# Other distances between the steps of the attention and mLSTM chains, matrix sums in threes, and another order of the first late sets in a hybrid decoder layer

## The chip, the cores and the metric

The kernel runs on one core of a Trainium2 chip. The metric is the device time of one execution in microseconds (us); the time before is the median of three runs. The trace is one profiled execution of the kernel before. Engines are called by the profile's names: PE multiplies matrices, PEld is its weight load, DVE and ACT do vector and scalar work, POOL a part of the vector work and some transfers, SP issues most transfers.

## What is computed

One decoder layer on 2048 tokens of width 1024, with 16 learned meta tokens in front. One input projection feeds two branches, which are gated, merged and projected:

```python
proj = u @ w_in
(a_q, a_k, a_v, a_z, m_qk, m_v, m_i, m_f, m_o, m_z, g_a, g_m) = split(proj)
att = sliding_window_attention_with_sinks(a_q, a_k, a_v)      # 16 heads, window 128, rope
y_a = (att * silu(a_z)) @ w_attn_out
m_q, m_k = split(silu(causal_conv(m_qk)))
cell = mlstm(m_q, m_k, m_v, m_i, m_f)                         # 4 heads, running state
hm = head_layernorm(sigmoid(m_o) * cell)
y_m = (hm * silu(m_z)) @ w_mlstm_out
out = rmsnorm((sigmoid(g_a) * y_a + sigmoid(g_m) * y_m) @ w_out) + x
```

All of it is float32. The kernel splits an operand into a high and a low part and multiplies three times (high by high, high by low, low by high).

## The kernel before

**Stage 1** goes through the tokens in two halves (c = 0 and 1) of 8 blocks of 128. In each half a plan lists projections: four times an A block (8 projections of q, k and v of a group of heads, `token_proj`, L756), an F block (4 projections for the mLSTM's q and k, `feat_proj`, L768) and an M block (8 projections of v and the output gate of an mLSTM head, L756 again); after the second and the fourth there is a block G of gates. A projection is 24 matmuls, of 512 columns in F and M and of 384 or 392 in A.

Between them stand the steps of **chains**, Python generators that a function `slot()` advances. A slot comes after each 6 projection matmuls: three within a projection, one behind it. What a generator yields is the number of slots until its next step. So the order on PE is written out by hand; the orders on DVE, ACT, POOL and SP come from a scheduler.

An **attention chain** treats a block of tokens and a group of heads. A new one starts every 12 slots at the earliest:

- three transposes of q and k (L440); ACT and DVE split them into `qs` and `ks` (L443 to L449);
- after `ATT_YIELDS[0]` slots the scores of the first two heads (L467, four matmuls into the tile `s`, two banks, one buffer); DVE masks (L469) and takes the row bounds (L473, L474), ACT takes the exponentials (L476) and thereby frees `s`;
- after `ATT_YIELDS[1]` slots the scores of the other two heads into the same buffer, L467 again;
- after `ATT_YIELDS[2]` slots the transposes of P (L492 and, for the meta columns, L493); ACT L496 and DVE L497 split them into `pc`, POOL masks (L501, L504) and spreads the meta part (`pmb`, L510);
- after `ATT_YIELDS[3]` slots P times V (L519, up to five matmuls); the result is stored to `att_d`.

In an M block each of 8 projections starts an **mLSTM chain**: a step T1 (L613 a transpose of k, L614 k times q) with its decay weights `dws` (ACT L627, DVE L628); after `ML_YIELDS[0]` slots the product with the state and the state's update (L587: six matmuls into `acc`, three into `su`, read by DVE L636); after `ML_YIELDS[1]` slots two transposes of the result (L652), which ACT L653 copies out.

L440, L492, T1, `su`, L652 and the meta keys' transposes (L411, L412) share one **PSUM pool of two buffers**, the tiles `tr`: each use waits until the engine that reads the use before the last is done with that buffer.

At the ends of the A blocks with index 1 and 3 the loop calls `slot()` without any matmul between the slots (**bare slots**) until enough chains are done: 57 of 813 slots.

`attn_meta` prepares the meta keys of a group once in each of the four A blocks of the first half: POOL turns them (rope, L281 to L284) and, after a `yield`, PE transposes them (L411, L412). `weight_sums` adds pairs of weight blocks in DRAM for the late stage, by transfers issued on ACT (`cp`) and POOL (`add`, L171), one per slot, with six matrices in all; some steps read what an earlier one has written.

**The late stage** has 12 sets (`SETS`), each with 7 products (`PRODS`) of 48 matmuls of 512 columns (L1144): a seven-product scheme for blocks of 2 by 2. A set's operands come from DRAM and are split by ACT (L965) and DVE (L966) into `st` and `r`; the tiles `r` of the tokens (from `uo_d`) are split in the first set of a half alone. A set's results go through a chain of DVE operations (L1035 to L1044, L1095 to L1100), much shorter for `gm` than for `az` and `mz`.

Of the kernel before, what the change touches and what calls it, by code (L numbers as in the profile page):

```python
# [35 lines left out]
NHALF = NB // HALF_BLOCKS  # L36
SBH = HALF_BLOCKS * 128 // SB
BIG = 1e30
ATT_YIELDS = (5, 5, 8, 9)
ML_YIELDS = (4, 6)  # L40
CHAIN_PHASE = 2
DMA_LEAD = 30
SPLIT_LEAD = 2
# [41 lines left out]
MATS = ("az", "mz", "gm", "att", "hm", "out")  # L85
# [3 lines left out]
def hybrid_layer(ctx: ExitStack, tc: tile.TileContext, x, xT, mx, mxT, gpre, w_all, wq, negs, cw, cb,  # L89
# [5 lines left out]
    def pool(name, bufs=1, space=None, es=ctx):  # L95
        kw = {} if space is None else {"space": space}
        return es.enter_context(tc.tile_pool(name=name, bufs=bufs, **kw))
# [16 lines left out]
    def f(t):  # L114
        return t.bitcast(F32)
# [62 lines left out]
                yield  # L178

    def weight_sums():  # L180
        for a in range(0, len(MATS), 2):
            pair = (a, a + 1)
            for op, i, src in ((cp, 2, (0, 0)), (cp, 0, (1, 1)), (add, 2, (0, 1)), (add, 0, (0, 1)),
                               (cp, 1, 2), (add, 1, (1, 1)), (cp, 3, 1), (add, 3, (1, 0))):
                for m in pair:
                    for j in range(2):
                        cs = slice(j * 2 * SB, (j + 1) * 2 * SB)
                        v = sw_d[m][src] if isinstance(src, int) else wq[m, src[0], src[1]]
                        op(sw_d[m][i][:, cs], v[:, cs])
                        yield  # L190
# [45 lines left out]
    with es1:  # L236
# [3 lines left out]
        def wt(name, shape, dt=F32, bufs=None):  # L240
            kw = {} if bufs is None else {"bufs": bufs}
            return wk.tile(shape, dt, name=name, **kw)
# [20 lines left out]
        def meta_proj(wh, wl, c0, n, dst):  # L263
            ps = ps_a.tile([128, SB], F32, name="acc")
            i = 0
            for k in range(KT):
                for w in (wh[k], wl[k]):
                    T.matmul(ps[0:48, :n], lhsT=um[:, k, :], rhs=w[:, c0:c0 + n],
                             start=(i == 0), stop=(i == 2 * KT - 1))
                    i += 1  # L270
            tmp = stage.tile([128, SB], F32, name="xs")
            S.copy(tmp[:NM, :n], ps[32:32 + NM, :n])
            tt(dst, ps[0:NM, :n], tmp[:NM, :n], ALU.add)

        def apply_rope(view, pos, nh, p):
            c = rope_t[:p, pos:pos + 1, 0:16].broadcast_to([p, nh, 16])
            sn = rope_t[:p, pos:pos + 1, 16:24].broadcast_to([p, nh, 8])
            sp = rope_t[:p, pos:pos + 1, 24:32].broadcast_to([p, nh, 8])
            a = wt("ropa", [128, 6, 16], bufs=1)
            b = wt("ropb", [128, 6, 16], bufs=1)  # L280
            G.tensor_tensor(a[:p, :nh], view[:, :, 0:16], c, ALU.mult)  # L281
            G.tensor_tensor(b[:p, :nh, 0:8], view[:, :, 8:16], sn, ALU.mult)
            G.tensor_tensor(b[:p, :nh, 8:16], view[:, :, 0:8], sp, ALU.mult)
            G.tensor_tensor(view[:, :, 0:16], a[:p, :nh], b[:p, :nh], ALU.add)  # L284
# [116 lines left out]
        def attn_meta(g, wh, wl, gt_raw):  # L401
            n = 136 if g == 0 else 128
            kv = stage.tile([128, SB], F32, name="xs")[:NM, 0:200]
            meta_proj(wh, wl, 256, n, kv[:, 64:64 + n])
            if g == 0:
                V.tensor_copy(gt_raw[0:NM, 0, :], kv[:, 192:200])
            V.tensor_copy(kv[:, 0:64], kv[:, 64:128])
            apply_rope(kv[:, 0:128].rearrange("p (a d) -> p a d", a=2), NB, 2, NM)
            yield 4
            tr = ps_t.tile([128, SB], F32, name="tr")  # L410
            T.transpose(out=tr[:, 0:NM], in_=kv[:, 0:128], identity=ident_t[:NM, :NM])  # L411
            T.matmul(tr[:, 64:128], lhsT=sel_t, rhs=kv[:, 128:192], start=True, stop=True)  # L412
            S.copy(KM[g][:, 0], tr[:, 0:NM])
            tt(KM[g][:, 1], tr[:, 0:NM], f(KM[g])[:, 0], ALU.subtract)
            S.copy(VM[g][:, 0:64], tr[:, 64:128])
            tt(VM[g][:, 64:128], tr[:, 64:128], f(VM[g])[:, 0:64], ALU.subtract)
# [20 lines left out]
        def attn_block(g, b, qkv, vt, vp, last):  # L437
# [18 lines left out]
            kring[0] = ks  # L456
            yield ATT_YIELDS[0]
            P = wt("P", [128, 4, 144], bufs=2)
            mn = wt("mn", [128, 16])
            c0 = 0 if b > 0 else 128  # L460
            for pr in range(2):
                if pr == 1:
                    yield ATT_YIELDS[1]
                sp = ps_s.tile([128, 2, SB], F32, name="s")
# [22 lines left out]
            tt(Pv[:, :, :, NM:], Pv[:, :, :, NM:], rv.broadcast_to([128, 2, 2, 128]), ALU.mult)  # L487
            yield ATT_YIELDS[2]
            tm = ps_a.tile([128, SB], F32, name="acc")
# [13 lines left out]
            for i in range(2):  # L503
# [7 lines left out]
                            bm_t.rearrange("p (s a) -> p s a", a=1).broadcast_to([128, 4, 128]), ALU.mult)  # L511
            yield ATT_YIELDS[3]
            ops = [(VM[g], pmb), (vt.rearrange("p a d -> p (a d)"), pc[:, 0]),
# [90 lines left out]
        def mlstm_chain(h, b, j, v1, tho, qT, kT, GT, mrep):  # L604
# [23 lines left out]
            tt(dws[:, 1], dw, f(dws)[:, 0], ALU.subtract)  # L628
            yield ML_YIELDS[0]
            acc = ps_a.tile([128, SB], F32, name="acc")  # L630
# [17 lines left out]
            S.activation(tho, tho, AF.Identity, bias=sm[:, 13:14], scale=sm[:, 11:12])  # L648
            yield ML_YIELDS[1]
            th = ps_t.tile([128, SB], F32, name="tr")  # L650
# [137 lines left out]
        u = [None, None]  # L788
        late = None
        sums.append(weight_sums())  # L790

        def first_proj(us, wh, wl, w):
# [12 lines left out]
        for c in range(NHALF):  # L805
# [7 lines left out]
            for pi, (kind, arg, cols) in enumerate(PLAN):  # L813
# [24 lines left out]
                if kind == "A":  # L838
                    chains = []
                    for i in range(HALF_BLOCKS):  # L840
# [28 lines left out]
                        if c == 0 and i == 6:  # L869
                            start(attn_meta(arg, wh, wl, gt_raw))  # L870
# [39 lines left out]
                else:  # L910
# [25 lines left out]
                    if un:  # L936
                        u = un
# [11 lines left out]
    NPAIR = SEQ // (2 * SB)  # L949
# [3 lines left out]
    ring = pool("ring", 1)  # L953
    ps_1 = pool("ps_1", 4, PSUM)
    ps_0 = pool("ps_0", 4, PSUM)
    SETS = [(n, c, ("u", c)) for c in range(NPAIR) for n in ("az", "mz", "gm")]
    SETS += [(n, c, ("w", n)) for n in ("att", "hm", "out") for c in range(NPAIR)]
    OPD = {"att": "att", "hm": "hm", "out": "mg"}
    IDX = {"P1": 0, "P2": 1, "P6": 2, "P5": 3, "P7": 4, "P3": 5, "P4": 6}

    def split(pl, nm, src, p, sign=1.0, bufs=None):
        raw = src.pop(0)
        op = pl.tile([128, 2, 2, SB], R, name=nm, **({} if bufs is None else {"bufs": bufs}))
        if sign == 1.0:
            S.copy(op[:, 0], raw)  # L965
            tt(op[:, 1], raw, f(op)[:, 0], ALU.subtract)  # L966
        else:
            S.activation(op[:, 0], raw, AF.Copy, scale=sign)
            stt(op[:, 1], raw, sign, f(op)[:, 0], ALU.mult, ALU.subtract)
        return op  # L970

    def weight_src(n, name):
        m = MATS.index(n)
        v = sw_d[m][int(name[1]) - 1] if name[0] == "s" else wq[m, int(name[1]), int(name[2])]
        return v.rearrange("p (k n) -> p k n", k=4)

    N = len(SETS) * NP
    fetched, ready, resident = {}, {}, {}

    def fetch(n):  # L980
        u, i = divmod(n, NP)
        nm, c, key = SETS[u]
        w_src = weight_src(nm, PRODS[i][2])
        b_src = (uo_d[c] if key[0] == "u" else op_d[OPD[nm], c])[i]
        srcs = [w_src, b_src] if key[0] == "u" else [b_src, w_src]
        if u and SETS[u - 1][2] == key:
            srcs.pop()
# [7 lines left out]
    def prep(n):  # L995
# [3 lines left out]
        if raws:  # L999
            sign = -1.0 if SETS[u][2][0] == "u" and PRODS[i][0] == "P6" else 1.0  # L1000
            resident[i] = [split(res if i else first, f"r{i}{p}", raws, p, sign) for p in range(2)]
# [119 lines left out]
    for n in range(N):  # L1121
        u, i = divmod(n, NP)
        nm, c, key = SETS[u]
        name, bset = PRODS[i][0], (PRODS[i][1] + u) % 2
# [94 lines left out]
```

## Time and profile before

| | us |
|---|---|
| median of three runs | 2472.01 (2469.97 to 2474.32) |
| the profiled execution, own time | 2472.98 |
| its span in the trace | 2469.8 |
| PE busy | 2305.6 (93%) |
| DVE, ACT, POOL busy | 1565.6, 1135.5, 635.0 |

The span is the time from the first to the last instruction that the profile shows; the execution's own time holds 3.2 us more. The granted clock (PEclk) is TensorE's as a share of full speed: 0.50 is 1.2 GHz, 1.00 is 2.4 GHz, and a stretch between them had a part at either. An idle time in square brackets stands before the instruction of its row, with what ended it.

### The profile page before, as it was taken

How to read it: one execution, taken by the hardware profiler on the slowest of the kernel's cores; microseconds unless marked ns; L12 is line 12 of the kernel's file. 1: busy time of each engine (PE TensorE's matmuls, PEld its weight loads, DVE VectorE, ACT ScalarE, POOL GpSimd, SP SyncE). 2: the span in 40 equal slices, each digit the busy share in tenths (PEclk: the TensorE clock that was granted, in tenths of full speed). 3: DMA queues.
4: the chain of work that ended last, by engine and by line, in shares of the span. 5: the costliest groups of instructions: out<-in, count | busy, mean ns of one | idle time of the engine just before them, and what ended most of it. 6: DMA issues, size and time to landing. Idle time of an engine off the chain costs nothing.

```text
span 2469.8 us, 34243 instructions
## 1 busy us (share of the span) xinstructions
PE 2305.6 (93%) x11149; PEld 1942.8 (79%) x11149; DVE 1565.6 (63%) x3371; ACT 1135.5 (46%) x2785; POOL 635.0 (26%) x1347
## 2 busy tenths in 40 slices
PE   7998889898998999999999997999999999989897
PEld 6787779687787878778788885788878888877686
DVE  7866654565766765754767755765587463666675
ACT  6554543454554454543555544444543442333342
POOL 5244344245342436343344430000000000000010
PEclk9999999999999999999999998999999999999999
DMA  7325445634468637445411117866797676889974
GB/s 231 126 63 147 97 94 114 150 90 122 98 152 224 167 91 140 107 94 122 120 46 56 43 48 238 285 228 221 253 296 222 212 258 214 283 272 304 285 264 151
DMA packets 216915, 415.51 MB, mean 168 GB/s; under 512 B 23212, under 2 KB 80896, under 8 KB 216736
## 3 DMA queue, kind: packets, MB, share of 16 engines
q1 hardware_dynamic: 200032, 352.51, 44.0%
q0 software_dynamic: 9792, 35.66, 9.7%
q10 hardware_dynamic: 6912, 25.17, 3.4%
q8 instruction: 87, 1.43, 0.2%
q14 instruction: 92, 0.75, 0.1%
HBM read 302.06 MB, written 172.00 MB: 192 GB/s over the span
## 4 chain that ended last, share of the span: by engine, by line
PE 41%; DVE 10%; DMA 8%; issue 3%; ACT 3%; POOL 2%; SPq 1%; ACTq 0%; DVEq 0%; POOLq 0%
PE x L1144 25%; PE pj L756 7%; PE pj L768 5%; DMA raw<-uo_d 2%; DMA wraw<-in_w_all 2%; PE acc L519 1%; DMA ld<-gm_d 1%; DVE st L966 1%; PE s L467 1%; DVE wlo L213 1%; DVE e L1085 1%; DMA raw<-sw_d 1%; DVE xs L531 1%; DMA hm_d<-tho 1%; ACT P L476 1%
## 5 line engine op out<-in xcount | busy, mean ns | idle before, releaser
L1144 PE MATMUL x<-r,st 128*128 128x512 f32 x2688 | 619.8, 393 | 29.2 <-DMA ld<-att_d 13.1
L756 PE MATMUL pj<-whi,un 128*128 128x512 f32 (+2 forms) x1952 | 636.1, 383 | 0.0
L1144 PEld LDWEIGHTS x<-r,st 128*128 128x128 f32 x2688 | 509.7, 190 | 139.4 <-ACT st L965 13.8
L756 PEld LDWEIGHTS pj<-whi,un 128*128 128x128 f32 x1952 | 375.1, 194 | 41.9 <-issue 2.3
L756 PE MATMUL pj<-wlo,un 128*128 128x512 f32 (+2 forms) x976 | 365.8, 375 | 4.7 <-DVE wlo L213 4.7
L768 PE MATMUL pj<-un,whi 128*128 128x512 f32 x1024 | 328.1, 402 | 1.2 <-ACT xs L542 1.2
L966 DVE TENSOR_TENSOR st<-raw,st 128x1024 fp32r<-128x1024 f32 x168 | 204.4, 1222 | 189.1 <-ACT st L965 182.5
L1144 PE MATMUL x<-st,r 128*128 128x512 f32 x1344 | 308.8, 392 | 9.1 <-DVE st L966 5.3
L965 ACT CAST st<-raw 128x1024 fp32r<-128x1024 f32 x168 | 176.2, 1052 | 290.6 <-PE x L1144 155.3
L1144 PEld LDWEIGHTS x<-st,r 128*128 128x128 f32 x1344 | 253.6, 189 | 64.2 <-DVE st L966 6.0
L1052 POOL TENSOR_TENSOR yss<-yss,mhalf 128x1 f32<-128x1 f32 x16 | 12.6, 795 | 959.1 <-DVE yss L1051 954.3
L768 PEld LDWEIGHTS pj<-un,whi 128*128 128x128 f32 x1024 | 188.6, 192 | 36.8 <-ACT xs L542 1.6
L756 PEld LDWEIGHTS pj<-wlo,un 128*128 128x128 f32 x976 | 190.5, 195 | 24.5 <-DVE wlo L213 7.9
L768 PE MATMUL pj<-un,wlo 128*128 128x512 f32 x512 | 202.8, 396 | 0.0
L476 ACT ACTIVATE P<-s,mn 128x144 f32<-128x144 f32 x256 | 95.2, 378 | 170.6 <-DVE mn L474 161.8
L213 DVE TENSOR_TENSOR wlo<-wraw,whi 128x512 fp32r<-128x512 f32 (+3 forms) x224 | 142.1, 657 | 27.2 <-ACT whi L212 26.2
L966 DVE TENSOR_TENSOR r<-raw,r 128x1024 fp32r<-128x1024 f32 x66 | 80.6, 1223 | 106.6 <-ACT r L965 106.4
L501 POOL TENSOR_SCALAR_AFFINE_SELECT pp<-pc 128x512 fp32r<-128x512 f32 x120 | 77.4, 646 | 247.1 <-ACT pc L496 240.2
L212 ACT CAST whi<-wraw 128x512 fp32r<-128x512 f32 (+3 forms) x224 | 110.8, 529 | 54.0 <-DMA wraw<-in_w_all 43.4
L965 ACT CAST r<-raw 128x1024 fp32r<-128x1024 f32 x66 | 69.4, 1051 | 116.5 <-DMA raw<-uo_d 45.6
L768 PEld LDWEIGHTS pj<-un,wlo 128*128 128x128 f32 x512 | 97.8, 191 | 21.9
L469 DVE COPY_PREDICATED s<-um,s 128x256 f32<-128x256 int32 x120 | 51.0, 425 | 98.2 <-PE s L467 97.8
(365 smaller groups left out, 3609.2 us busy)
## 6 DMA issues: line engine op xcount, KB each, us to landing
raw<-sw_d SPq DMA_DIRECT2D x72, 512.0 KB, 5.8
raw<-in_wq SPq DMA_DIRECT2D x54, 512.0 KB, 4.5
wraw<-in_w_all SPq DMA_DIRECT2D x96, 256.0 KB, 3.9
sw_d<-in_wq POOLq DMA_DIRECT2D x48, 512.0 KB, 7.3
raw<-uo_d SPq DMA_DIRECT2D x28, 512.0 KB, 4.9
raw<-op_att_d SPq DMA_DIRECT2D x28, 512.0 KB, 5.5
raw<-op_hm_d SPq DMA_DIRECT2D x28, 512.0 KB, 6.0
raw<-op_mg_d SPq DMA_DIRECT2D x28, 512.0 KB, 5.3
```

What stands on the lines that cost most here:

```text
L212: S.copy(hi[:, :w], raw[:, :w])
L213: tt(lo[:, :w], raw[:, :w], f(hi)[:, :w], ALU.subtract)
L467: T.matmul(sp[:, pa, c0:272], lhsT=qs[:, pr, pa, :], rhs=ks[:, i, c0:272], start=(i == 0), stop=(i == 1))
L469: V.copy_predicated(sp[:, :, 144:272], um_t.rearrange("p (a t) -> p a t", a=1).broadcast_to([128, 2, 128]), sp[:, :, 0:128] if b > 0 else ...
L476: S.activation(P[:, 2 * pa + pr], sp[:, pa, 128:272], AF.Exp, bias=mn[:, 2 * pr + pa:2 * pr + pa + 1], scale=-1.0, accum_out=mn[:, 4 + 2 * ...
L501: G.affine_select(pp[:, i], f(pc)[:, i], pattern=[[0, 4], [-1, 128]], compare_op=ALU.is_gt, fill=0.0, base=0, channel_multiplier=1)
L519: T.matmul(acc, lhsT=l, rhs=r.rearrange("p s q -> p (s q)"), start=(i == 0), stop=(i == len(ops) - 1))
L756: T.matmul(ps[:, :w], lhsT=us[k][:, a, o:o + 128], rhs=ww[k][:, :w], start=(n == 0), stop=(n == 3 * KT - 1))
L768: T.matmul(ps, lhsT=ww[k][:, 128 * i:128 * i + 128], rhs=us[k][:, a], start=(n == 0), stop=(n == 3 * KT - 1))
L965: S.copy(op[:, 0], raw)
L966: tt(op[:, 1], raw, f(op)[:, 0], ALU.subtract)
L1144: T.matmul(banks[bset][g], lhsT=l, rhs=r, start=(fresh and p == 0 and kk == 0 and m == 0), stop=(p == 1 and kk == 1 and m == 2), skip_grou ...
```

## The change

Six lines change. Of the attention chain's distances the first grows by two slots, the second shrinks by two and the third grows by one; both distances of the mLSTM chain shrink by one. `weight_sums` goes through three matrices at once (the variable is still called `pair`). The meta keys' transposes come 8 slots behind their rope instead of 4. In the first half the late sets run gm, az, mz.

```diff
-ATT_YIELDS = (5, 5, 8, 9)
-ML_YIELDS = (4, 6)
+ATT_YIELDS = (7, 3, 9, 9)
+ML_YIELDS = (3, 5)
...
     def weight_sums():
-        for a in range(0, len(MATS), 2):
-            pair = (a, a + 1)
+        for a in range(0, len(MATS), 3):
+            pair = range(a, a + 3)
...
             apply_rope(kv[:, 0:128].rearrange("p (a d) -> p a d", a=2), NB, 2, NM)
-            yield 4
+            yield 8
...
-    SETS = [(n, c, ("u", c)) for c in range(NPAIR) for n in ("az", "mz", "gm")]
+    SETS = [(n, c, ("u", c)) for c in range(NPAIR) for n in (("az", "mz", "gm") if c else ("gm", "az", "mz"))]
```

The first place is PE in the first M block of the second half, around the q and k transposes (L440) of an attention chain. `su` is written by the L587 that name `tr`, `DVE_49` and `Activation_49` are semaphores of those engines. Before:

```order
L587 MATMUL tr<-v_7605,kw 128x258 [waits PE_49]
L587 MATMUL tr<-v_7605,kw 128x258 x2
L613 MATMUL tr<-ident,kT 128x128
L614 MATMUL tr<-qT,kT 128x128
L756 MATMUL pj<-whi,un 128x512
L756 MATMUL pj<-wlo,un 128x512
L756 MATMUL pj<-whi,un 128x512 x2
L756 MATMUL pj<-wlo,un 128x512
L756 MATMUL pj<-whi,un 128x512
L440 MATMUL tr<-ident,qkv 128x128 [waits DVE_49]
```

The same chains in the changed kernel:

```order
L587 MATMUL tr<-v_7629,kw 128x258 [waits PE_49]
L587 MATMUL tr<-v_7629,kw 128x258 x2
L756 MATMUL pj<-whi,un 128x512
L756 MATMUL pj<-wlo,un 128x512
L756 MATMUL pj<-whi,un 128x512 x2
L756 MATMUL pj<-wlo,un 128x512
L756 MATMUL pj<-whi,un 128x512
L652 MATMUL tr<-ident,tho 128x128 x2
L613 MATMUL tr<-ident,kT 128x128 [waits DVE_49]
L614 MATMUL tr<-qT,kT 128x128
L440 MATMUL tr<-ident,qkv 128x128 [waits Activation_49]
```

T1 has moved from behind `su` to one slot later, into the slot of L652 and L440; L440, which waited for DVE's reading of `su` over 6 projection matmuls, now waits for ACT's copy of the L652 two rows above it. Such a wait of L440 stands in 14 places of the changed kernel.

The second place is PE at the end of the second A block of the second half, where bare slots begin. Before:

```order
L467 MATMUL s<-ks,qs 128x272 [waits DVE_49,PE_49,Activation_49]
L467 MATMUL s<-ks,qs 128x272 x3
L756 MATMUL pj<-whi,un 128x384
L756 MATMUL pj<-wlo,un 128x384
L756 MATMUL pj<-whi,un 128x384 x2
L756 MATMUL pj<-wlo,un 128x384
L756 MATMUL pj<-whi,un 128x384
L440 MATMUL tr<-ident,qkv 128x128 x3
L519 MATMUL acc<-pmb,vm_197 128x512 [waits Pool_49]
```

In the changed kernel:

```order
L492 MATMUL tr<-ident,P 128x128 x4
L493 MATMUL acc<-ident,Pm 64x128 [waits Pool_49]
L467 MATMUL s<-ks,qs 128x272 [waits Activation_49]
L467 MATMUL s<-ks,qs 128x272 [waits DVE_49]
L467 MATMUL s<-ks,qs 128x272 x2
L756 MATMUL pj<-whi,un 128x384
L756 MATMUL pj<-wlo,un 128x384
L756 MATMUL pj<-whi,un 128x384 x2
L756 MATMUL pj<-wlo,un 128x384
L756 MATMUL pj<-whi,un 128x384
L467 MATMUL s<-ks,qs 128x272 [waits DVE_49,PE_49,Activation_49]
L467 MATMUL s<-ks,qs 128x272 x3
```

Between the transposes of P and the P·V behind these rows (L519) stood 30 projection matmuls before, and 6 now; both pairs of scores of the next chain have come in between. The same holds at the end of the fourth A block of that half. In the whole of stage 1, 66 of 822 slots are bare.

The third place is DVE in the late stage at the end of the set `mz` of the first half, where the splits of the next set's operands (L966) follow the last operations on results. Before, with `gm` as the next set:

```order
L1095 SCALAR_TENSOR_TENSOR th<-th,x 128x512
L966 TENSOR_TENSOR st<-raw,st 128x1024
L1100 SCALAR_TENSOR_TENSOR bt<-ld,hn,th 128x512
L966 TENSOR_TENSOR st<-raw,st 128x1024
L1044 SCALAR_TENSOR_TENSOR b_18150<-b_18150,bt 128x512
L966 TENSOR_TENSOR st<-raw,st 128x1024 x3
```

In the changed kernel, with `az` of the second half next:

```order
L1095 SCALAR_TENSOR_TENSOR th<-th,x 128x512 x2
L1100 SCALAR_TENSOR_TENSOR bt<-ld,hn,th 128x512 x2
L1044 SCALAR_TENSOR_TENSOR b_18639<-b_18639,bt 128x512
L1044 SCALAR_TENSOR_TENSOR b_18648<-b_18648,bt 128x512
L966 TENSOR_TENSOR st<-raw,st 128x1024 x2
L966 TENSOR_TENSOR r_18891<-raw,r_18891 128x1024
L966 TENSOR_TENSOR r_18894<-raw,r_18894 128x1024
L966 TENSOR_TENSOR st<-raw,st 128x1024 x2
```

The splits have moved behind the last L1100 and L1044, and two splits of `r` stand among them.

## Rows read from the trace of the kernel before

**Rows 1.** Two stretches: busy per engine (instructions), granted clock, DMA share, GB/s

```profile
0.00:1489.00 1489.00, 1377.35 (x7117) 1179.54 (x7117) 952.19 (x2571) 738.99 (x2241) 622.38 (x1331) 0.96 0.45 115
...
1502.20:2194.00 691.80, 685.51 (x3001) 565.96 (x3002) 422.15 (x521) 297.14 (x386) 0.00 (x0) 0.99 0.75 246
```

**Rows 2.** Waits of PE, 0 to 1490: who for whom, total, times, longest

```profile
PE tr L613 <- DVE pc L497: 14.5, 11, 2.9
PE tr L411 <- POOL xs L284: 14.4, 4, 4.4
PE acc L519 <- POOL pmb L510: 13.8, 5, 4.2
PE tr L613 <- DVE ks L449: 8.8, 4, 3.4
PE s L467 <- ACT ks L448: 7.9, 4, 4.6
...
PE tr L440 <- DVE cst L636: 5.6, 7, 1.8
PE s L467 <- ACT P L476: 4.9, 3, 2.8
...
PE s L467 <- DVE ks L449: 2.3, 4, 1.0
```

**Rows 3.** A stretch of 16 us around a P·V wait, columns as in rows 1

```profile
192.00:208.00 16.00, 12.90 (x68) 12.05 (x67) 8.55 (x23) 5.88 (x25) 5.47 (x12) 0.79 0.35 109
```

**Rows 4.** Two stretches of 16 us around waits of T1 and L467

```profile
484.00:500.00 16.00, 13.25 (x55) 10.36 (x56) 9.74 (x28) 6.82 (x21) 4.93 (x10) 0.79 0.30 62
...
756.00:772.00 16.00, 11.41 (x50) 9.53 (x50) 6.67 (x17) 4.76 (x13) 3.60 (x6) 0.89 1.05 321
```

**Rows 5.** The same columns, 1210 to 1226

```profile
1210.00:1226.00 16.00, 10.67 (x53) 8.07 (x52) 10.79 (x29) 7.46 (x26) 5.65 (x10) 1.00 0.27 80
```

**Rows 6.** Timeline of PE: start, duration, line, operation, count [idle before <- releaser]

```profile
1081.93 0.33 PE L613 MATMUL tr<-ident,kT 128*128 128x128 f32 x1 [1.59 <-DVE pc L497]
...
1083.03 0.62 PE L768 MATMUL pj<-un,whi 128*128 128x512 f32 x2
...
1083.72 0.62 PE L768 MATMUL pj<-un,whi 128*128 128x512 f32 x2
```

**Rows 7.** L652: count, min/median/max ns, first and last start

```profile
L652 PE MATMUL tr<-ident,tho x128: 270/271/473, 119.8 to 1446.8; 128*128 128x128 f32 x128
```

**Rows 8.** L653, the copy behind it, same columns

```profile
L653 ACT COPY tho<-tr x64: 347/372/380, 121.1 to 1447.2; 128x256 f32<-128x256 f32 x64
```

**Rows 9.** L467, the scores

```profile
L467 PE MATMUL s<-ks,qs x512: 228/288/594, 81.6 to 1469.2; 128*128 128x272 f32 x160, 128*128 128x144 f32 x11
```

**Rows 10.** L476, the exponentials

```profile
L476 ACT ACTIVATE P<-s,mn x256: 359/380/408, 85.3 to 1471.1; 128x144 f32<-128x144 f32 x128
```

**Rows 11.** L613, the first matmul of T1

```profile
L613 PE MATMUL tr<-ident,kT x64: 270/273/477, 99.4 to 1428.3; 128*128 128x128 f32 x64
```

**Rows 12.** L628, the decay weights

```profile
L628 DVE TENSOR_TENSOR dws<-dw,dws x64: 409/425/1268, 101.7 to 1432.9; 128x256 fp32r<-128x256 f32 x64
```

**Rows 13.** Timeline of POOL, the sums of weights in DRAM

```profile
1192.83 0.81 POOL L171 DMA_DIRECT2D sw_d<-in_wq  x1 [5.32 <-DMA sw_d<-sw_d]
```

**Rows 14.** Timeline of PE at the first meta keys

```profile
52.62 0.23 PE L411 MATMUL tr<-ident,xs 16*128 16x16 f32 x1 [3.45 <-POOL xs L284]
...
57.22 0.45 PE L268 MATMUL acc<-whi,umeta 128*48 128x256 f32 x1 [1.86 <-ACT whi L212]
```

**Rows 15.** Timeline of PE, late stage, 1502 to 1850: the rows with idle time

```profile
1502.10 90.86 PE L1144 MATMUL x<-r,st 128*128 128x512 f32 x386 [13.12 <-DMA ld<-att_d]
1596.87 230.40 PE L1144 MATMUL x<-r,st 128*128 128x512 f32 x1008 [3.91 <-DVE st L966]
1829.60 20.69 PE L1144 MATMUL x<-r,st 128*128 128x512 f32 x90 [2.33 <-DVE st L966]
```

**Rows 16.** Timeline of DVE ahead of the second of these waits

```profile
1595.60 1.22 DVE L966 TENSOR_TENSOR st<-raw,st 128x1024 fp32r<-128x1024 f32 x1
```

## What I predict, and why

> **What bounds the kernel now.** I read first the stretches by stage: PE is busy 1377 of the first 1489 us, so stage 1 loses 112 us, and 685.5 of the 691.8 us that follow its end, so most of the late stage loses 6 [rows 1]. PE is the bound throughout; only what lets PE wait, or lowers its clock, moves the end. Next the waits of PE in stage 1: they are many kinds of a few us each [rows 2], and the change touches nearly all of them by moving the point in PE's order at which the wait stands. Third the granted clock around such waits: after some it falls to 0.50 for a while, and a stretch of 16 us then has a mean of 0.79 or 0.89 [rows 3, 4]; around three waits that follow each other in 1210 to 1226 it stays at 1.00 [rows 5]. So a wait has two prices, its idle time and the matmuls at half clock behind it. Last the timelines of the late stage's rows with idle time [rows 15].
>
> The profiled execution took 2472.98 us, 1 us above the median; its span of 2469.8 leaves 3.2 us outside, which nothing here touches. I make the sum against 2472.98. In the M and F blocks a projection matmul of 512 columns costs 0.23 us (three from 1083.03 to 1083.72 [rows 6]): a slot is 1.4 us, three slots 4.1.
>
> **The chains: what goes.** (a) T1 waits for DVE's L497 because the transposes of P stand just ahead of it in the ring of two `tr` buffers: 14.5 us in 11 [rows 2], as at 1081.93 [rows 6]. In the changed order `su` and L652 stand between them. I take all of it, -14.5; if some of it comes back as a wait for the use that now precedes, -10. (b) T1 waits for L449, the split of k: 8.8 in 4, the longest 3.4 [rows 2]. The distance from L440 grows from 18 to 24 matmuls, that is by 1.4 us: two waits of 3.4 lose 1.4 each and two of about 1.0 vanish, -4.8 (bounds -2.8 and -5.5). (c) The first scores wait for `ks`, 7.9 in 4 on ACT and 2.3 in 4 on DVE [rows 2]; two slots more give 2.8 us, which leaves 1.8 of the longest (4.6): -8.4 (bounds -6 and -10.2). (d) L440 waits for DVE's L636, 5.6 in 7 [rows 2]. That goes, but T1 now stands 6 matmuls behind each `su` as L440 did: I put a wait of the same 5.6 in its place, so 0. (e) Clock: around the waits of (a) to (c) nine stretches of 16 us have a lowered clock, five at 0.79 and four at 0.89 (one of each in rows 4). They lose up to 5 x 16 x 0.21 + 4 x 16 x 0.11 = 24 us of full-speed time, less the idle part. Since the longest waits of (b) and (c) shrink and do not all vanish, I take -14, with bounds 0 and -20.
>
> **The chains: what comes.** (f) In 14 places L440 now needs the buffer of an L652 in the same slot, with only T1 between (L613 takes 0.27 us [rows 11]). From the first and last of 64 pairs, an L652 starts at 119.8 and its copy ends 0.37 after 121.1, 1.7 later; 1446.8 and 1447.2 give 0.8 [rows 7, 8]. Less 0.3 for T1 this leaves 0.5 to 1.4 for each, 7 to 19 in all. I take 9, near the low end, since such short waits leave the clock alone [rows 5]; queued behind L440 is PE's whole order. (g) The second scores stand 18 matmuls (4.1 us) behind the first, not 30, and need the second exponential of the first. From the first scores to that exponential it takes 3.7 us plus two of 0.38 and their read-outs at 81.6, and 2.0 plus the same at 1469.1 [rows 9, 10]: between nothing and a short wait in the two end pairs. All 64 pairs taken so give 21 us over 18 matmuls, in 10 of them, and 5 over 30, as the trace shows (4.9 in 3 [rows 2]). So it adds 0 to 16. (h) L587 stands 18 matmuls behind T1, not 24. T1 to the end of L628 takes 2.7 us in the first pair and 5.0 in the last [rows 11, 12]; over all 64 the excess beyond 18 matmuls is 22 us in 10, beyond 24 it is 4.5. So 0 to 17. The largest of (g) and of (h) are the same two backlogs, at 856 to 860 and at 1205 to 1209, and PE waits one out only once; I take 8 and 6. (i) Two P·V that had 30 matmuls between them and their transposes have 6, in bare slots. Five such waits cost 13.8 now, 2.8 each [rows 2], and the clock behind one costs 16 x 0.21 = 3.4 [rows 3]: 2 x 6.0 = +12 (bounds 6 and 12).
>
> Chains: -14.5 - 4.8 - 8.4 - 14 + 9 + 8 + 6 + 12 = -6.7.
>
> A rule of the Trainium skill speaks against the change here. The trace first: three waits within 10 us left the clock at 1.00 [rows 5], single waits of 3 us lowered it [rows 3, 4]. The Trainium skill, page "TensorE: Matmul & The Clock Gate", section "A second HAM failure mode: psum-queue depth-cycling", describes a kernel that cycles through PSUM banks with many tiny pauses between groups of matmuls and pays for the clock toggling. By that rule the 14 bunched places would each lower the clock; the trace so far agrees for long waits alone.
>
> **Rope and sums.** (j) The four waits of L411 cost 14.4, the longest 4.4 [rows 2]. The first, 3.45, goes, but the next block's weights are late anyway: L268 waits for ACT's cast 4 us on [rows 14], and that cast stays behind the same work. Two, of nearly 4.4, stand in bare slots, which hold no matmul: four slots more of them give nothing. The last, 14.4 - 3.45 - 8.8 = 2.2, goes: -2.2 (bounds 0 and -5). (k) The sums' transfers wait for each other on POOL, up to 5.32 us at 1192.83 [rows 13], and the masks and casts of the chains are queued behind. In threes six transfers stand between dependent ones and not four. The exponentials that PE waits for nearby cost 4.9 in all [rows 2]: -2 (0 to -5).
>
> **Late stage.** (l) The gap of 13.12 at the start [rows 15] stays: the first products of `gm` read the same kind of operands at the same places of SP's, ACT's and DVE's order as those of `az` did, behind the last stores of attention. (m) The wait at 1596.87, 3.91, is one for splits that DVE reaches only behind the quarters of `az` [rows 15, 16]; it stays with `az` to `mz`, perhaps smaller because the splits of `r` now fall into the light `gm`: -2 (0 to -3.9). (n) `mz` of the first half was followed by the light `gm`, without a wait. It is now followed by `az` of the second half, whose splits stand behind all of `mz`'s last operations, and two splits of `r` of 1.22 us [rows 16] with them. Between 2.33 and 3.91 [rows 15], plus 2.4: I take 4.5 (2 to 6). Late: +2.5.
>
> Sum: 2472.98 - 6.7 - 2.2 - 2 + 2.5 = 2464.6, say **2464.5**.
>
> **Rivals.** *The short distances cost more* (slower). Mechanism: ACT and DVE serve the chains in the same order as the weights' casts, so the tails of (f), (g) and (h) come at their full price: +10, +8 and +11 over what I took, and some clock behind the longest, up to 10, gives 2503. It decides from about 12 us on, where the kernel is slower by 0.2%; half of the price with half of the clock gives 2484, its typical time 2488. For it: the tails are in the trace. Against it: they overlap, and short waits do not touch the clock. *Each wait is replaced by another* (no change): the uses of the ring stay as many, and T1 waits for `su` or L652 in place of L497 with the old clock behind it; (a), (e) lose 17 of their 28.5, and less comes in (f) to (h), 13 in place of 23: 2472. For it: (d) is such a case, and (j) has another. Against it: the new neighbours' readers are shorter than L496 with L497. *The clock toggles* at the 14 bunched places: 3.4 each [rows 4] is 48 us over my sum, 2512. Rows 5 speak against it; this is the rule of the Trainium skill above. That the change does nothing for the sums or the meta keys is inside (j) and (k), since bounds there reach 0.
>
> **How the numbers follow.** A measurement of this kernel can tell about 0.2%, 5 us, from no change. Forecast: 0.47, with 2445 to 2467 as its own range. Slower by the short distances: 0.28; clock toggling: 0.03; together slower 0.31. Replaced: 0.22. With every term at its better end the time would be about 2425, at its worse end 2534; not all of them fall to one side, so about 60% of the way down and some 45% up, 2440 to 2495, leaves 0.07 below and 0.13 above.
>
> **What would show it.** In the changed profile: no row "L613 waits for L497" above 3 us in total (a), and granted clock 1.00 in the M blocks of the first half (e); a row of L440 waiting for ACT's L653 with about 14 times 0.7 (f); L467 waiting for L476 with 10 to 15 in place of 4.9 (g); L587 waiting for L628 with 5 to 10 (h); seven waits or so of L519 for L510 (i); L1144 after 1650 with one new wait of 4 to 5 for L966 (n), and 13 still at the start (l). The forecast is wrong if L467 and L587 together wait over 30, or if the clock falls in blocks in which it is at 1.00 now.

## The result, and the profile after

The changed kernel takes 2455.99 us (2453.92 to 2461.08), the kernel before 2472.01: the ratio is 0.9944, with a 95% interval from 0.9920 to 0.9968, so 16 us faster. The forecast was 2464.5, with a range from 2440 to 2495.

The gain is all in stage 1. There the first late product starts at 1475.77, not at 1502.10 [rows 15], 26 us earlier; from that product to the end of the span it then takes 978.4 us and not 967.7, 11 more. The waits of PE in stage 1, who for whom, total, times, longest, answer [rows 2]:

```profile
PE s L467 <- ACT P L476: 25.6, 18, 3.2
...
PE tr L613 <- DVE cst L636: 9.8, 16, 1.1
PE acc L268 <- ACT whi L212: 9.6, 3, 4.5
PE acc L268 <- DVE wlo L213: 8.4, 7, 4.4
PE tr L440 <- ACT tho L653: 5.7, 15, 0.4
PE tr L411 <- POOL xs L284: 4.5, 2, 2.6
PE acc L587 <- ACT dws L627: 4.0, 7, 1.8
PE acc L519 <- POOL pmb L510: 4.0, 3, 2.5
...
PE pj L768 <- ACT xs L781: 2.5, 1, 2.5
...
PE tr L613 <- DVE pc L497: 2.2, 3, 0.7
...
PE tr L613 <- DVE ks L449: 1.9, 1, 1.9
```

Four rows of the kernel before, of the same view as [rows 2], that are needed below:

```profile
PE tr L652 <- DVE cst L636: 5.7, 2, 3.2
...
PE tr L613 <- DVE cst L636: 3.7, 2, 2.2
PE acc L268 <- ACT whi L212: 2.5, 2, 1.9
...
PE acc L268 <- DVE wlo L213: 1.6, 4, 0.5
```

T1's wait for L497 has gone from 14.5 to 2.2, and most of the waits for `ks` and for P·V have gone too; the largest row is now the second scores' wait for the exponentials. The M block around the first stretch of [rows 4] has its full clock back (columns as in rows 1: length, busy per engine, granted clock, DMA share, GB/s). Before:

```profile
473.60:549.60 76.00, 69.94 (x362) 57.15 (x360) 51.82 (x156) 44.17 (x132) 28.78 (x68) 0.96 0.37 95
```

The same block in the changed kernel, and a stretch with short waits:

```profile
462.90:531.80 68.90, 66.31 (x363) 55.55 (x360) 49.44 (x150) 39.68 (x120) 28.13 (x69) 1.00 0.40 105
...
1192.00:1208.00 16.00, 14.73 (x77) 11.90 (x76) 10.94 (x39) 8.42 (x29) 6.89 (x20) 1.00 0.06 17
```

The second stretch of [rows 4] lies in a G block, and that block did not get its clock back: before, it was at half clock for 3.4 us from 760.66, behind a wait of 4.59 for `ks`; now it is so for 3.4 us from 744.59, behind the wait of 2.5 for ACT's L781 in the rows above.

In the stretch with short waits lie a wait of T1 and one of L440, as the timeline of PE shows:

```profile
1199.74 0.33 PE L613 MATMUL tr<-ident,kT 128*128 128x128 f32 x1 [0.71 <-DVE cst L636]
...
1200.73 0.55 PE L440 MATMUL tr<-ident,qkv 128*128 128x128 f32 x3 [0.43 <-ACT tho L653]
```

The late stage's rows with idle time up to 1900 (against [rows 15]):

```profile
1475.77 242.92 PE L1144 MATMUL x<-r,st 128*128 128x512 f32 x1057 [12.60 <-ACT st L965]
1723.76 78.47 PE L1144 MATMUL x<-r,st 128*128 128x512 f32 x337 [5.07 <-DVE r L966]
1808.99 91.25 PE L1144 MATMUL x<-r,st 128*128 128x512 f32 x393 [6.75 <-DVE st L966]
```

The wait behind the first `az` has gone; there is a new one of 5.07 where `az` of the second half follows `mz` of the first, and the one behind that `az` has grown from 2.33 to 6.75.

**Where the time of stage 1 went, by kind of block.** A single profile of stage 1 scatters by several us, mostly in A and F (the two profiles of the changed kernel are the second row below). The M blocks scatter less: each sum below runs from a block's first projection matmul to the first of the block behind it, for M over eight blocks, and the eight profiles of kernels with the distances 7-3-9-9 and 3-5, three of them in the table, have 563.5 to 570.2 us there. The other rows are one profile each.

| kernel | distances | A | F | M | G |
|---|---|---|---|---|---|
| before | 5-5-8-9, 4-6 | 432 | 214 | 605 | 227 |
| changed, and once more | 7-3-9-9, 3-5 | 441, 438 | 221, 219 | 570, 570 | 220, 220 |
| late sets in the old order | 7-3-9-9, 3-5 | 444 | 228 | 570 | 220 |
| mLSTM distances new, attention's old | 5-5-8-9, 3-5 | 434 | 225 | 600 | 222 |
| attention distances new, mLSTM's old | 7-3-9-9, 4-6 | 441 | 230 | 598 | 225 |
| first scores a slot earlier | 6-4-9-9, 3-5 | 441 | 219 | 580 | 223 |
| second scores a slot later | 7-4-8-9, 3-5 | 433 | 213 | 590 | 220 |

The M blocks lose 35 us and G loses 7; A and F give some 15 back.

### The profile page after: what moved, and what is told of

Its sections match the earlier page's. It is cut to its first block, busy times and chain, and to the rows that moved or that the text cites. A ratio compares the mean times of both kernels' runs of the same rounds, so it can differ in the third digit from the quotient of the medians.

```text
span 2454.2 us, 34263 instructions
## 1 busy us (share of the span) xinstructions
PE 2297.4 (94%) x11149; PEld 1934.7 (79%) x11149; DVE 1556.4 (63%) x3371; ACT 1140.5 (46%) x2785; POOL 626.5 (26%) x1347
## 4 chain that ended last, share of the span: by engine, by line
PE 47%; DVE 14%; DMA 9%; ACT 4%; issue 4%; POOL 3%; SPq 1%; ACTq 0%; DVEq 0%; POOLq 0%
PE x L1144 25%; PE pj L756 9%; PE pj L768 7%; PE acc L519 2%; DMA raw<-uo_d 2%; DMA wraw<-in_w_all 1%; DVE wlo L213 1%; DMA ld<-part_d 1%; DVE xs L531 1%; PE s L467 1%; DVE st L966 1%; DMA raw<-sw_d 1%; DMA ld<-gm_d 1%; ACT P L476 1%; PE acc L587 1%
## 5 line engine op out<-in xcount | busy, mean ns | idle before, releaser
L1144 PE MATMUL x<-r,st 128*128 128x512 f32 x2688 | 623.2, 394 | 33.4 <-ACT st L965 12.6
L1144 PEld LDWEIGHTS x<-r,st 128*128 128x128 f32 x2688 | 512.6, 191 | 144.1 <-ACT st L965 13.3
L756 PE MATMUL pj<-whi,un 128*128 128x512 f32 (+2 forms) x1952 | 607.8, 373 | 0.0
L756 PEld LDWEIGHTS pj<-whi,un 128*128 128x128 f32 x1952 | 366.6, 190 | 40.1 <-issue 1.7
L756 PE MATMUL pj<-wlo,un 128*128 128x512 f32 (+2 forms) x976 | 359.0, 368 | 3.0 <-DVE wlo L213 3.0
L966 DVE TENSOR_TENSOR st<-raw,st 128x1024 fp32r<-128x1024 f32 x168 | 204.2, 1222 | 201.9 <-ACT st L965 196.7
L1144 PE MATMUL x<-st,r 128*128 128x512 f32 x1344 | 310.6, 394 | 9.1 <-DVE st L966 4.5
L1144 PEld LDWEIGHTS x<-st,r 128*128 128x128 f32 x1344 | 255.4, 190 | 64.2 <-DVE st L966 4.9
L966 DVE TENSOR_TENSOR r<-raw,r 128x1024 fp32r<-128x1024 f32 x66 | 80.5, 1223 | 107.3 <-ACT r L965 107.1
L476 ACT ACTIVATE P<-s,mn 128x144 f32<-128x144 f32 x256 | 95.4, 379 | 113.9 <-DVE mn L474 112.3
L467 PE MATMUL s<-ks,qs 128*128 128x272 f32 (+1 forms) x512 | 93.6, 305 | 26.5 <-ACT P L476 25.6
```

The costliest lines, as they stand in the source:

```text
L467: T.matmul(sp[:, pa, c0:272], lhsT=qs[:, pr, pa, :], rhs=ks[:, i, c0:272], start=(i == 0), stop=(i == 1))
L476: S.activation(P[:, 2 * pa + pr], sp[:, pa, 128:272], AF.Exp, bias=mn[:, 2 * pr + pa:2 * pr + pa + 1], scale=-1.0, accum_out=mn[:, 4 + 2 * ...
L756: T.matmul(ps[:, :w], lhsT=us[k][:, a, o:o + 128], rhs=ww[k][:, :w], start=(n == 0), stop=(n == 3 * KT - 1))
L1144: T.matmul(banks[bset][g], lhsT=l, rhs=r, start=(fresh and p == 0 and kk == 0 and m == 0), stop=(p == 1 and kk == 1 and m == 2), skip_grou ...
```

## The experiments

All ratios are to the kernel before on the same chip, each with its 95% interval. The runs stand on three chips, where the kernel before took 2470.0 us (a0 to a3), 2470.8 (a4 to a6 and b1) and 2471.4 (d1 to d4). A name in brackets is a run's; the expectations use these names.

**The late sets' order and the meta keys.** As a yardstick the changed kernel once more (a0_after):

> The changed kernel once more, as the yardstick for the next three: 2453 to 2459 us, 13 to 19 us below the kernel before.

It took 2455.4 us, ratio 0.9949 (0.9932 to 0.9967). Then the old order of the sets (a1_gm_back):

```diff
-    SETS = [(n, c, ("u", c)) for c in range(NPAIR) for n in (("az", "mz", "gm") if c else ("gm", "az", "mz"))]
+    SETS = [(n, c, ("u", c)) for c in range(NPAIR) for n in ("az", "mz", "gm")]
```

> The changed kernel with the late sets of the first half in the old order (az, mz, gm). Theory 1 (four heavy sets in a row let DVE fall behind): the waits of 5.1 us at mz to az and of 6.8 at az to mz of the second half go, those of 3.9 and 2.3 come back, and the clock behind them falls for one spell of 3.4 us, not two of 6.8: 8 to 12 us faster than the changed kernel, about 2446. Theory 2 (the late stage loses its 10 us because stage 1 ends at another moment, whatever the order of the sets): within 3 us of the changed kernel, 2453 to 2459.

Measured: 2451.1, ratio 0.9929 (0.9910 to 0.9948). Its late waits, in the timeline of PE:

```profile
1582.32 79.21 PE L1144 MATMUL x<-r,st 128*128 128x512 f32 x336 [4.99 <-DVE st L966]
1662.10 152.64 PE L1144 MATMUL x<-r,st 128*128 128x512 f32 x672 [0.56 <-DVE st L966]
1816.55 142.89 PE L1144 MATMUL x<-r,st 128*128 128x512 f32 x622 [1.81 <-DVE st L966]
```

They sum to 7.4, not 11.8. Over all profiles the late stage, from the first L1144 to the end of the span, takes 975.9 to 981.1 us (mean 978.4) in six profiles with the new order and 967.7 to 974.8 (mean 971.2) in six with the old: the order costs 7 us there. In the time only 4 us show, and the intervals overlap. The waits have gone where theory 1 said, and its amount (8 to 12) was too high; its reason, heavy sets in a row, is tested further below. The meta keys (a2_meta_back):

```diff
-            yield 8
+            yield 4
             tr = ps_t.tile([128, SB], F32, name="tr")
```

> The changed kernel with the meta keys' transposes 4 slots behind their rope again. Theory 1 (the 8 slots put them, and the casts of weights queued behind, too late): PE's waits for the rope L284 rise from 4.5 to about 14 us, those of L268 for ACT and DVE fall from 18 to about 4: 2 to 7 us faster than the changed kernel. Theory 2 (L268 waits for its weights because of the chains' new steps): L268 keeps its 18 us and the rope's waits come on top: 5 to 10 us slower.

Measured: 2456.7, ratio 0.9947 (0.9930 to 0.9965), no difference. Its waits:

```profile
PE tr L411 <- POOL xs L284: 10.3, 4, 3.0
...
PE acc L268 <- DVE wlo L213: 4.8, 8, 1.1
...
PE acc L268 <- ACT whi L212: 2.5, 2, 1.9
```

L268 falls from 18.0 to 7.3 as theory 1 says, but L411 takes 6 of that back, and the time does not tell the two apart. Theory 2 is out. Both undone (a3_gm_meta_back):

> Both undone at once. By the first theory of each: the two gains add, 10 to 18 us faster than the changed kernel, 2438 to 2447, the fastest of all so far. By the second: within 8 us of the changed kernel.

Measured: 2449.5, ratio 0.9929 (0.9909 to 0.9949): 6 us under the yardstick. That is the number of the second theories, but with intervals of this width it does not exclude the lower end of the first.

**The sums**, in pairs again (a6_sums_back):

```diff
-        for a in range(0, len(MATS), 3):
-            pair = range(a, a + 3)
+        for a in range(0, len(MATS), 2):
+            pair = (a, a + 1)
```

> The changed kernel with the sums of matrices in pairs again. My term was 2 us (0 to 5): 0 to 5 us slower than the changed kernel, with waits of POOL for sw_d of 15 to 25 us in total against fewer in the changed kernel. Rival: no difference, since POOL is idle most of the time and none of its waits is on PE's path: within 1.5 us.

Measured: 2457.3, ratio 0.9944 (0.9927 to 0.9961), no difference. POOL's waits for the sums were 18.9 us in 3 before, are 1.1 in 1 in the changed kernel and 4.3 in 1 here, the 15 to 25 expected did not come back. So the long waits of before were no fixed cost of pairs. Whether one of them delayed PE in the kernel before, no run shows.

**The distances alone**, in the kernel before, with all else of before (b1_att_ml):

```diff
-ATT_YIELDS = (5, 5, 8, 9)
-ML_YIELDS = (4, 6)
+ATT_YIELDS = (7, 3, 9, 9)
+ML_YIELDS = (3, 5)
```

> The kernel before with both new sets of distances and nothing else. Theory 1 (the distances bring more than the whole change does, the other parts cost some 10 us): 24 to 34 us faster than the kernel before, 2438 to 2448, within 4 us of the run with the late sets and the meta keys undone. Theory 2 (the parts need each other): 10 to 20 us faster.

Measured: 2456.0, ratio 0.9941 (0.9923 to 0.9958), the same as the whole change. The other three parts together bring nothing that can be measured. Theory 1 expected ten us more and fell.

**One pair of distances without the other.** In the changed kernel the attention distances of before (a4_att_back):

```diff
-ATT_YIELDS = (7, 3, 9, 9)
+ATT_YIELDS = (5, 5, 8, 9)
```

> The changed kernel with the attention distances of before (5, 5, 8, 9) and the new mLSTM ones (3, 5). Theory 1 (it is the mLSTM distances that take T1 away from the transposes of P, and with it the clock): T1 waits for L497 stay near 2 us; L467 waits for L476 fall from 25.6 to about 5, P.V for POOL rise from 4 to about 14, L467 waits for ks rise from 1 to about 10: within 8 us of the changed kernel, 2449 to 2464. Theory 2 (the attention distances carry the gain): 12 us slower or more, near the kernel before.

Measured: 2486.7, ratio 1.0069 (1.0048 to 1.0089), 31 us above the yardstick and slower than before. Its M blocks take 600 us. Its first late product starts at 1505.39, only 3 us behind that of the kernel before; the rest of its loss against that kernel lies in the late stage, which it has in the new order (979.4 us against 967.7). Theory 1 fell: T1's wait for L497 went up to 6.7 only, but L652 now waits for the same split:

```profile
PE acc L519 <- POOL pmb L510: 14.5, 6, 3.1
...
PE tr L652 <- DVE pc L497: 13.1, 10, 2.1
...
PE acc L587 <- ACT dws L627: 8.3, 8, 1.8
...
PE tr L587 <- DVE mn L478: 8.1, 3, 3.8
PE s L467 <- ACT P L476: 7.1, 3, 4.3
```

And in the changed kernel the mLSTM distances of before (a5_ml_back):

```diff
-ML_YIELDS = (3, 5)
+ML_YIELDS = (4, 6)
```

> The changed kernel with the mLSTM distances of before (4, 6) and the new attention ones. In its order T1 stands again in the slot of su, and in every second chain L440 in the same slot behind both. Theory 1: the buffers of the ring are reused at once, T1, L652 and L440 wait 25 to 40 us in all, and the clock falls in the M blocks again: 12 to 30 us slower than the changed kernel. Theory 2 (the attention distances carry the gain): within 6 us of the changed kernel.

Measured: 2495.6, ratio 1.0107 (1.0085 to 1.0128), 40 us above the yardstick. Here T1 stands in the slot of `su` and L440 right behind both, and waits for the reader of `su` (the changed kernel has 5.7 in 15, for L653):

```profile
PE tr L440 <- DVE cst L636: 34.9, 15, 3.2
```

One of them:

```profile
1036.02 0.52 PE L587 MATMUL tr<-v,kw 128*128 128x258 f32 x3
1036.38 0.27 PE L613 MATMUL tr<-ident,kT 128*128 128x128 f32 x1
1036.49 0.39 PE L614 MATMUL tr<-qT,kT 128*128 128x128 f32 x2
1040.07 0.59 PE L440 MATMUL tr<-ident,qkv 128*128 128x128 f32 x3 [3.19 <-DVE cst L636]
```

Theory 1 holds for the place. Its sizes were too small: L440, T1 and L652 wait some 50 us in all and not 25 to 40, and the time is 10 us above its range.

**What the attention distances do.** In the changed kernel's M blocks the first scores of a chain stand in the slot of the transposes of P of the chain before, behind them; with 5-5-8-9 they stand one slot ahead. A stretch of ACT in the run with the old attention distances (start, duration, line, operation):

```profile
511.04 0.38 ACT L476 ACTIVATE P<-s,mn 128x144 f32<-128x144 f32 x1 [1.21 <-DVE mn L474]
...
511.41 0.37 ACT L476 ACTIVATE P<-s,mn 128x144 f32<-128x144 f32 x1
...
511.76 0.58 ACT L496 CAST pc<-tr 128x512 fp32r<-128x512 f32 x1
```

PE started the scores at 506.95 and the transposes at 508.84. ACT waits for DVE's bounds of the scores, takes two exponentials, and only then splits `pc`, 2.9 us behind the transposes' start; L652 on PE, which wants the buffer, waits until 513.12. At the same step of the changed kernel the transposes start at 501.50, the scores follow, and ACT splits `pc` 1.1 us behind the transposes' start and takes the exponentials later:

```profile
502.62 0.56 ACT L496 CAST pc<-tr 128x512 fp32r<-128x512 f32 x1
...
505.94 0.39 ACT L476 ACTIVATE P<-s,mn 128x144 f32<-128x144 f32 x1
```

To test it, only the first scores were moved, one slot earlier, in the kernel with the old order of sets (d4_score_early):

```diff
-ATT_YIELDS = (7, 3, 9, 9)
+ATT_YIELDS = (6, 4, 9, 9)
```

> The changed kernel with the old order of late sets (the run a1_gm_back) and attention distances 6, 4, 9, 9: of all the chains' steps only the first scores move, one slot earlier, ahead of the transposes of P of the chain before, not behind them. Theory 1 (the order of arrival on ACT and DVE decides: scores that come first put their mask, bounds and exponentials ahead of the split of the transposed P, and T1 and L652 wait for that split): the time from L492 to the end of L497 rises from 2.2 us to about 3, PE's waits for L497 from 4 to 15 us or more, in spite of a gain of up to 8 us on the second scores: 5 to 20 us slower than a1_gm_back. Theory 2 (distances alone count): the second scores have 24 matmuls and not 18 behind the first, waits of L467 for L476 fall by 10 us, 5 to 10 us faster.

Measured: 2461.4, ratio 0.9955 (0.9934 to 0.9976). From the end of L492 to the end of L497 it now takes 2.65 us in the mean of 64 (2.17 in a1_gm_back), the waits for L497 are 10 us, and the M blocks take 580, 10 more, although the second scores' wait has all but gone:

```profile
PE acc L519 <- POOL pmb L510: 18.9, 7, 3.1
...
PE tr L613 <- DVE pc L497: 5.7, 7, 1.2
...
PE tr L652 <- DVE pc L497: 4.5, 6, 1.1
...
PE s L467 <- ACT P L476: 2.9, 1, 2.9
```

Theory 1 is right on the place and its waits are half as large as expected; the ratios' intervals overlap, so the time alone does not prove it. The row of L519 shows that in the bare slots the wait only changes its name, since in a1_gm_back these two rows were:

```profile
PE s L467 <- ACT P L476: 29.5, 19, 4.1
...
PE acc L519 <- POOL pmb L510: 4.9, 3, 3.4
```

That is 26 us off the second scores and 14 on P·V. Then only the second scores were moved, one slot later (d1_pair4):

```diff
-ATT_YIELDS = (7, 3, 9, 9)
+ATT_YIELDS = (7, 4, 8, 9)
```

> The run a1_gm_back with attention distances 7, 4, 8, 9: only the second scores move, one slot later, into the slot of the product with the state. Theory 1 (the remaining waits of L467 for L476, 25 to 32 us, are the price of the short distance): they fall to 10 to 18, 5 to 12 us faster than a1_gm_back. Theory 2 (the exponentials then meet the mLSTM's work on ACT and DVE, and others wait): L613, L440 and L587 wait 6 us more in all, within 4 us of it.

Measured: 2457.7, ratio 0.9955 (0.9938 to 0.9973), no faster. Their wait falls to 17.5 and the F blocks take 213 us, where kernels with the distance of 3 take 219 to 232, but the M blocks take 590, 20 more: PE's idle time there rises from 33 to 48 us and the time at half clock from 7 to 24. The second scores now share the slot with the product with the state, and it is L587 and L440 that wait longer (L587 for `dws` 6.2 and L440 5.4 in a1_gm_back):

```profile
PE s L467 <- ACT P L476: 17.5, 11, 2.1
...
PE acc L587 <- ACT dws L627: 10.6, 9, 2.2
...
PE tr L440 <- ACT tho L653: 8.1, 14, 0.8
...
PE tr L587 <- DVE mn L478: 7.5, 3, 3.2
```

So theory 2 holds on the place: L613, L440 and L587 wait some 4 us more in all. The time is 6 us above that of a1_gm_back, not within 4, with intervals that overlap. Against the changed kernel's 570 us in the M blocks the first scores a slot earlier cost 10, the second a slot later 20, and both with L440 a slot later, which is 5-5-8-9, cost 30.

**A light set between heavy ones**, alone (d2_apart) and with 7-4-8-9 (d3_both):

```diff
-    SETS = [(n, c, ("u", c)) for c in range(NPAIR) for n in ("az", "mz", "gm")]
+    SETS = [(n, c, ("u", c)) for c in range(NPAIR) for n in (("gm", "az", "mz") if c else ("az", "gm", "mz"))]
```

> The run a1_gm_back with the late sets as az, gm, mz in the first half and gm, az, mz in the second, so that a light set stands between heavy ones but for the last pair. Theory 1 (a wait comes where a heavy set follows a heavy one): the wait of 4 to 6 us at 1577 to 1582 of that run goes, the last one (2 to 5) stays, and a spell of low clock with it: 4 to 8 us faster. Rival (gm needs as much of DVE as the others for the splits of r): a wait of the same size at another place, within 2 us.

> The order of sets of d2_apart and the distances of d1_pair4 together. By the first theory of each: 9 to 20 us faster than a1_gm_back, about 2437; by the second: within 5 us of it.

Measured: 2458.4, ratio 0.9949 (0.9932 to 0.9965), and with 7-4-8-9 2466.9, ratio 0.9991 (0.9974 to 1.0007). Neither is a gain, and the second is a loss that neither theory of its expectation has: 15 us above a1_gm_back, with intervals that do not meet. On one chip and with intervals apart, it is 9 us slower than d1_pair4, which has the same distances and the old order of sets (late stage 977.7 us against 968.8), and 8 us slower than d2_apart, which has the same order of sets (M blocks 590 against 570). In the first the waits are 4.67 at 1572.36, between `az` and `gm`, and, between `mz` and `gm` and between the last `mz` and the first set behind it,

```profile
1733.38 220.25 PE L1144 MATMUL x<-r,st 128*128 128x512 f32 x959 [5.74 <-DVE r L966]
1967.71 0.79 PE L1144 MATMUL x<-st,r 128*128 128x512 f32 x1 [2.98 <-DVE st L966]
```

So it isn't heavy next to heavy that makes the wait: each of these stands behind a heavy set, ahead of whatever comes, and the one pair of heavy neighbours, `az` to `mz` in the second half, has none. With the heavy sets apart the late stage takes 983.4 and 977.7 us, no less than the 975.9 to 981.1 with four in a row. The order on DVE does not decide it alone: at `az` to `mz` DVE has the splits behind the last quarters as at `az` to `gm`, but comes to the first of them 9.6 us behind the set's first product and not 14.9. What makes DVE late in one place and not in the other is not shown.

None of these versions is shown to be faster than the changed kernel: the two lowest, with the late sets in the old order, lie 4 and 6 us under it, with intervals that overlap.

## Why the prediction was right, and where its terms were off

The direction, the range and the main mechanism held: waits for the ring's buffers, and the clock behind them, outweigh what the shorter distances add. By the steps, all from one profile of each kernel, waits by their labels:

| step | predicted | measured |
|---|---|---|
| (a) T1 for L497 | -14.5 | -12.3 (14.5 to 2.2) |
| (b) T1 for L449 | -4.8 | -6.9 (8.8 to 1.9) |
| (c) first scores for `ks` | -8.4 | -9.4 (10.2 to 0.8) |
| (d) L440 for `su`, then T1 for it | 0 | +0.5 (-5.6; T1 from 3.7 to 9.8) |
| (e) clock | -14 | -20 (half clock 105 to 65 us up to the last gates) |
| (f) L440 for L653 | +9 | +5.7, 0.4 each in 15 |
| (g) second scores, outside bare slots | +8 | +6.5 |
| (h) L587 for `dws` | +6 | +1.7 |
| (i) P·V in bare slots | +12 | about +4 |
| (j) meta keys | -2.2 | +4 (L411 -9.9, L268 +13.9) |
| (k) sums | -2 | 0 |
| (l) to (n) late | +2.5 | +11 here, +7 in the mean of profiles |

The column adds up to -15 and the two profiles differ by 17. It is no full account: L652's waits for `su` and `dw`, 6.9 in 3 before, are gone but for 1.0 in 2, and no term has them.

**Luck in the sum.** The chains were to give 6.7 us and gave some 30; the meta keys, the sums and the late stage were to give 1.7 and cost some 15. The forecast came within 9 us because these errors have opposite signs.

**The signs.** Of those named ahead, T1 for L497 (2.2), the new wait of (n) and the start of the late stage came as said, and L440 for L653 came in 15 places but at 0.4. L467 for L476 (25.6, not 10 to 15), L587 for `dws` (4.3, not 5 to 10) and L519 (three waits, not seven) did not, and one M block of the first half is not at full clock (half clock for 6.8 us from 270.14). The signs of being wrong were met or all but met: L467 for L476 and L587 for `dws` wait 29.9 us with a limit of 30, and 33.5 with all that the two wait for; and the clock fell for 3.4 us at 963.05 in an F block that was at 1.00 before, behind a wait of L467 of 3.19. The time held all the same because (b), (c), (e) and (i) came out better than their terms.

**Mis-sized terms.** (i) is the largest in stage 1. I saw that P·V would follow its transposes in 6 matmuls at two more places, and priced two more waits. I did not price that the second scores, which stand between, have a wait of their own (2.00, 1.09 and so on, eight rows with 14.2 us), and that it runs while POOL makes `pmb`, as here, where L510 ends at 936.30:

```profile
935.67 1.24 PE L467 MATMUL s<-ks,qs 128*128 128x272 f32 x4 [2.00 <-ACT P L476]
...
937.21 0.78 PE L519 MATMUL acc<-pmb,vm 128*128 128x512 f32 x1
```

P·V itself waits 4.0, not 13.8. The two rows sum to 18.2 against 13.8, and so (i) is about 4, its clock apart, which the table has under (e); of the 25.6 us in the second scores' row only 11.4 lie elsewhere. (e) was right in kind and too careful: in the M blocks the half clock fell from 43 to 7 us. (f) was taken near its low end and came out below it; from the end of L652 to the end of its copy it now takes 1.32 us in the mean of 64, 1.71 before. Three readings were off: the smaller waits of (b) were 1.85 and 0.15, not two of 1.0, which makes -4.4 by its own reckoning; the last starts in rows 9 and 10 belong to a chain's second scores, so the end pair of (g) is not the one meant; and the terms' bounds add up to 2424 and 2524, not 2534.

**Late stage.** (l) and the 4.5 of (n) were right (12.60; 5.07). What I missed is the set behind: there, at `az` to `mz` of the second half, PE waits 6.75, not 2.33, and the clock, for which (n) had nothing, falls for 6.8 us at each of the two. The gain of (m) came in full, 3.9.

**The sign of (j)** was wrong: I had L268's delay as a reason for no gain, and it grew to more than the gain. In the time it is not to be seen.

**The rivals.** The short distances do cost in single steps, but (f) to (h) sum to 14, not 23. That is what the rival of replaced waits had for them (13), but (a) and (e) did not shrink as it had it. The clock does not toggle at the bunched places: 1.00 in 1192 to 1208 with two waits of this kind. The Trainium skill, page "TensorE: Matmul & The Clock Gate", section "A second HAM failure mode: psum-queue depth-cycling", describes a clock that toggles with frequent tiny pauses; for waits of 0.4 to 0.7 us at these places the trace disagrees with that rule as the prediction applied it.

**What was right for an incomplete reason.** I added the two sets of distances up as if each brought its own gains. Neither does: each alone leaves the M blocks at some 600 us, where both together reach 570. For the mLSTM side the cause is shown (T1 in the slot of `su`, L440 right behind). For the attention side the two moves of the scores, each alone, cost 10 and 20 us, as much as the 30 of 5-5-8-9; L440's move was not made alone, so that the sum fits can be chance. That the first acts by the order on ACT is shown in the rows above; of the second only that the waits of L587 and L440 grow and the clock falls.

## What to carry to other kernels

Where several chains share a ring of buffers and the queues of the evicting engines, look at what stands next to what in one period of the order, not at each distance: a step that hands a buffer on should reach PE just ahead of the step whose readers are slow, not behind, as the transposes of P ahead of the scores here. A wait in a stretch without filler work moves to the next step when its own is shortened, so price the stretch, not the row. And before a sum over parts is trusted, ask whether two of them set the same position: here neither pair of distances without the other brought the M blocks below some 600 us, where both together reach 570.

## What the runs showed that I had not expected

Short waits are cheap: the M blocks of the changed kernel have waits of up to 1.6 us each, and but for one (1.9 at 269.2) none was followed by half clock, so that the same number of projection matmuls took 35 us less while PE's idle time there fell by some 20 only (51 to 32 us). The rest is the clock. In a4_att_back it is the other way round: its M blocks have 55 us of idle time in many waits of mostly under 1.7 us and only 15 us at half clock, and take 600 us all the same. So a wait is not to be judged by its clock alone.

The same kernel's stage 1 ended between 1470.8 and 1475.8 us in two profiles, with its M blocks at 570 in both; what scatters are the A and F blocks, and why is not shown. Comparing kinds of blocks told apart kernels that the times alone did not.
